# LayerNorm ahead of two feed-forwards: sums from the residual add and ScalarE's squares in place of VectorE's batch-norm statistics

## The chip, the cores and the metric

The kernel runs on one core of one Trainium2 chip. The metric is the device time of one execution in microseconds (us). The kernel before took 2121.43 us (median of three runs, 2121.37 to 2122.96). The engines are named as in the profile: PE is TensorE's matrix multiplication and PEld its weight load, DVE is VectorE, ACT is ScalarE, POOL is GpSimd, SP is the engine whose queue issues most of the DMAs.

## The reference

A decoder of two layers on 1024 positions of width 1024, all in float32. Each layer is a token mixer (a gated linear recurrence in the first, sliding-window attention in the second) and a gated feed-forward with a convolution of width 3. After the mixer and after the feed-forward stands a residual sum with a LayerNorm. The change touches the LayerNorm between mixer and feed-forward, once in each layer:

```
def layer_norm(x, g, b):
    mu = xf.mean(-1, keepdims=True)
    var = jnp.square(xf - mu).mean(-1, keepdims=True)
    y = (xf - mu) * lax.rsqrt(var + LN_EPS) * g + b

for layer in range(DEPTH):
    mix = ...
    h = layer_norm(ALPHA * h + mix, ln_mix_g[layer], ln_mix_b[layer])
    ff = conv_ffn(h, ffn_w_in[layer], ffn_conv_w[layer], ffn_conv_b[layer], ffn_w_out[layer])
    h = layer_norm(ALPHA * h + ff, ln_ffn_g[layer], ln_ffn_b[layer])
```

## The kernel before

Float32 products are computed as three matrix products of a high and a low part (`mm3`, lines 222 to 224). The high part is a cast on ScalarE (line 249) and the low part a subtraction on VectorE (line 197), so every operand costs both engines an operation. The 1024 positions are eight blocks of 128 (`tb` 0 to 7), one position to a partition; a block's 1024 features lie in its row of `Y`.

The entry of a feed-forward is `out_proj`. It multiplies the mixer's output by its output weights in two passes over the blocks: first the left 512 columns for blocks 0 to 7, then the right 512 columns for blocks 4, 5, 6, 7, 0, 1, 2, 3. Each half is a group of 24 matrix products into one PSUM bank (`psmm`, a pool of four banks). At its end VectorE adds it to ALPHA times the residual (line 380, here called the block's sum) and so frees the bank, and takes batch-norm statistics of that half (line 263). After the right half follows the norm of that block, `Up.ln`: aggregate the statistics (line 269), add the epsilon (line 270), raise to the power -1/2 on GpSimd (line 271), subtract the mean and multiply by `g` (line 280, the first pass), multiply by the root and add `b` (line 283, the second pass). Some 8 to 13 us later by the planner's count, TensorE transposes the block (line 232) into two more PSUM banks, from which ScalarE and VectorE make the high and low parts of `T`; sums of parts that the feed-forward's fast matrix multiplication needs come from lines 433 to 445. Between these stand the first weights of the feed-forward: loads on SP, casts on ScalarE, sums on VectorE (lines 480 to 483).

The order of TensorE's work is written out by hand through `Order`, which steps generators as its own clock `t` advances. The order of ScalarE's, VectorE's, GpSimd's and SP's work in the entries is set by the framework's scheduler, which goes by its own costs; operations in `urgent()` come ahead of others. Each engine then runs its list strictly in order.

Of the kernel before, what the change touches and what calls it, by code (L numbers as in the profile page):

```python
# [10 lines left out]
F32 = mybir.dt.float32  # L11
# [5 lines left out]
P = 128  # L17
S = 1024
D = 1024
# [115 lines left out]
def trunk(ctx: ExitStack, tc: tile.TileContext, a: dict, out: bass.AP):  # L135
# [123 lines left out]
    def ln_half(tb, i):  # L259

        if tb not in half_stats:
            half_stats[tb] = sm.tile([P, 2, 6], F32, name="st", bufs=8)
        nc.vector.bn_stats(half_stats[tb][:, i, :], Y[:, tb, i * 512:(i + 1) * 512])  # L263
# [7 lines left out]
        nc.gpsimd.tensor_tensor(rs, rs, nhalf, op=ALU.pow)  # L271
        return mv, rs

    def ln_affine(tb, rows, dst, n=1):

        y = Y[:, tb, :]
        mv, rs = ln_stats(tb)
        parts = [slice(h * D // n, (h + 1) * D // n) for h in range(n)]
        for hs in parts:
            nc.vector.scalar_tensor_tensor(y[:, hs], y[:, hs], mv[:, 0:1], rows[0][:, hs],  # L280
                                           op0=ALU.subtract, op1=ALU.mult)
        for hs in parts:
            nc.vector.scalar_tensor_tensor(y[:, hs], y[:, hs], rs, rows[1][:, hs], op0=ALU.mult, op1=ALU.add)  # L283
            nc.sync.dma_start(dst(hs), y[:, hs])
# [71 lines left out]
    def out_proj(us, begun, rows, resid, ff, ln):  # L356
        tasks, late = [], []
        for tb in range(NB):
            nc.sync.dma_start(Y[:, tb, :], resid(tb))
        for tb, ps in enumerate(begun):  # L360
            out_part(ps, us, tb, [KC - 1])
        for dh in range(2):
            if dh:
                ff.row_loads()
                ff.weights(1)
            for tb in range(NB):
                if dh == 0 and tb < 4:
                    out_late(late, rows, tb, ff.TX)
                elif dh == 0 and tb == 4:
                    ff.weights(0)  # L370
                if dh:
                    tb = (tb + 4) % NB
                if dh == 0 and tb < len(begun):
                    ps = begun[tb]
                else:
                    ps = psmm()
                    out_part(ps, late if dh else us, tb, range(KC))
                y = Y[:, tb, dh * 512:(dh + 1) * 512]
                with urgent() if dh else nullcontext():
                    nc.vector.scalar_tensor_tensor(y, y, ALPHA, ps, op0=ALU.mult, op1=ALU.add)  # L380
                    ln_half(tb, dh)
                if dh == 1:
                    tasks.append(od.spawn(ln(tb)))
                    od.tick()
        return tasks
# [17 lines left out]
    class Up:  # L403
        def __init__(self, l, pool, rx):
            self.l, self.rx = l, rx
            self.wv = a["ffn_w_in"][l].rearrange("(kc p) c -> p kc c", p=P)
            self.TX = pool.tile([P, 2, 2, 4, 512], F32R, name="TX")
            self.T2 = pool.tile([P, 2, 4, 512], F32R, name="T2")
            self.W, self.raw, self.pieces = {}, {}, 0

        def row_loads(self):
# [5 lines left out]

        def ln(self, tb):
            with urgent():
                ln_affine(tb, self.rows, lambda hs: ynd[:, tb, hs], 2 if tb == 3 else 1)  # L420
            yield 8.0 if tb < 4 else 10.0 if self.l else 13.0
            turned = lambda t: (self.rx[2 * t - 4] if t in (2, 3) else Y[:, t, :]).rearrange("p (k t) -> p k t", k=KC)
            hf = turned(tb)
            ts = slice(tb * P, (tb + 1) * P)
            with urgent():
                for q in range(2):
                    ps, ks = psmm(), slice(4 * q, 4 * q + 4)
                    for k in range(4):
                        tr(ps[:, k * P:(k + 1) * P], Y[:, tb, (4 * q + k) * P:(4 * q + k + 1) * P])
                    pv = ps.rearrange("p (k t) -> p k t", k=4)  # L430
                    if tb < 4:
                        split(T[:, 0, ks, ts], T[:, 1, ks, ts], pv)
                        nc.scalar.copy(hf[:, ks], pv)
                    elif q == 0:
                        nc.scalar.copy(hf[:, ks], pv)
                    else:
                        split(T[:, 0, ks, ts], T[:, 1, ks, ts], pv)
                        tt(hf[:, ks], hf[:, :4], pv, op=add)
                        split(T[:, 0, :4, ts], T[:, 1, :4, ts], hf[:, ks])
                        return  # L440
            sf = turned(tb + 4)
            a11, a12, a21, s1 = hf[:, :4], hf[:, 4:], sf[:, :4], sf[:, 4:]
            tt(a21, a11, a21, op=sub)
            tt(a11, s1, a11, op=sub)
            tt(a12, a12, a11, op=sub)
            split(self.T2[:, 0, :, ts], self.T2[:, 1, :, ts], a21)
            yield 100.0
            pair = hf.rearrange("p (c k) t -> p c k t", c=2)
            split(self.TX[:, :, 0, :, ts], self.TX[:, :, 1, :, ts], pair)
# [1462 lines left out]
```

## Time and profile before

| | us |
|---|---|
| median of three runs | 2121.43 |
| the profiled execution | 2122.24 |
| its span, first to last instruction | 2120.4 |
| first entry, blocks' norms | about 498 to 555 from the span's start |
| second entry, blocks' norms | about 1437 to 1490 |

The profiled execution took 0.8 us more than the median. The page gives each engine's busy time, the chain of work that ended last and the costliest groups of instructions. A row of a group has the line of the kernel, the engine, the operation, output and inputs, the shape, the count, busy time, the mean in ns, and the idle time of the engine just before these instructions with what ended it. A row in order of time has its start, its duration, the engine, the line and the operation; in brackets stands how long the engine had been idle and for what.

### The profile page before, as it was taken

Reading aid. Unit: us, or ns where it says so; the run is one execution under the profiler, and the core shown is the slowest. Engines: PE = TensorE matmul, PEld = TensorE weight load, DVE = VectorE, ACT = ScalarE, POOL = GpSimd, SP = SyncE. Lnnn points to the kernel's source line nnn. Section 1 sums busy time; section 2 is a strip of 40 time slices with the busy share of each in tenths; the row PEclk is TensorE's granted clock in tenths of the full one; section 3 lists DMA queues with packets and bytes.
Section 4 is the critical chain, followed back from the end, with each engine's and each line's share of the span. In section 5 each row is a group of like instructions: output and inputs, shape, how many; then the busy total and the mean of one; then the engine's idle time right before and its main releaser. Section 6 shows DMA issues by size and latency. Waiting matters only on the chain. (4 is left out here: it accounts for less than half of the span.)

```text
span 2120.4 us, 31566 instructions
## 1 busy us (share of the span) xinstructions
PE 2091.9 (99%) x12303; PEld 1742.8 (82%) x12303; DVE 1777.2 (84%) x2420; ACT 968.1 (46%) x1562; POOL 187.1 (9%) x214
## 2 busy tenths in 40 slices
PE   9899999999999999999999999999999999999998
PEld 7688888887878888888888888888888888888886
DVE  6677777769989999888988668979999999978986
ACT  6455565543444444444433356743544444444430
POOL 1000000001010000000001122311010000000002
PEclk9999999999999999999999999999999999999999
DMA  4021111143247765628754511052266776449662
GB/s 153 21 71 50 51 51 51 66 169 110 90 124 174 194 156 150 157 98 294 268 189 159 159 34 38 23 156 93 85 167 167 177 174 161 123 152 326 225 207 98
DMA packets 239823, 286.82 MB, mean 135 GB/s; under 512 B 30216, under 2 KB 160440, under 8 KB 239416
## 3 DMA queue, kind: packets, MB, share of 16 engines
q1 hardware_dynamic: 223360, 238.26, 34.6%
q0 software_dynamic: 15456, 46.16, 10.9%
q8 instruction: 97, 1.59, 0.3%
q14 instruction: 54, 0.44, 0.1%
q10 hardware_dynamic: 856, 0.37, 0.1%
HBM read 241.72 MB, written 89.15 MB: 156 GB/s over the span
## 5 line engine op out<-in xcount | busy, mean ns | idle before, releaser
L222 PE MATMUL psmm<-T,HL 128*128 128x512 f32 x816 | 323.3, 396 | 5.2 <-ACT T L874 4.8
L223 PE MATMUL psmm<-T,HL 128*128 128x512 f32 x816 | 319.2, 391 | 1.3 <-DVE T L197 1.3
L224 PE MATMUL psmm<-T,HL 128*128 128x512 f32 x816 | 319.3, 391 | 0.2 <-DVE HL L197 0.2
L528 DVE SCALAR_TENSOR_TENSOR Y<-Y,cwt,Y 128x1023 f32<-128x1023 f32 (+1 forms) x176 | 225.1, 1281 | 49.7 <-ACT Y L526 48.3
L249 ACT CAST HL<-rx 128x1024 fp32r<-128x1024 f32 (+1 forms) x151 | 151.1, 1006 | 159.6 <-DMA rx<-in_ffn_w_in_dram 28.1
L197 DVE TENSOR_TENSOR HL<-rx,HL 128x1024 fp32r<-128x1024 f32 (+1 forms) x151 | 176.4, 1175 | 17.6 <-ACT HL L249 17.3
L222 PEld LDWEIGHTS psmm<-T,HL 128*128 128x128 f32 x816 | 153.9, 189 | 36.8 <-ACT T L874 5.2
L224 PEld LDWEIGHTS psmm<-T,HL 128*128 128x128 f32 x816 | 153.8, 188 | 33.0 <-DVE HL L197 0.6
L223 PEld LDWEIGHTS psmm<-T,HL 128*128 128x128 f32 x816 | 153.9, 189 | 32.8 <-DVE T L197 2.2
L222 PE MATMUL psax<-T,HL 128*128 128x512 f32 x392 | 153.5, 392 | 0.0
L223 PE MATMUL psax<-T,HL 128*128 128x512 f32 x392 | 152.9, 390 | 0.0
L224 PE MATMUL psax<-T,HL 128*128 128x512 f32 x392 | 152.7, 390 | 0.0
L526 ACT ACTIVATE Y<-Y,cwt 128x1024 f32<-128x1024 f32 x88 | 108.8, 1237 | 92.8 <-DVE Y L515 82.8
L197 DVE TENSOR_TENSOR HL<-raw,HL 128x512 fp32r<-128x512 f32 (+1 forms) x121 | 92.2, 789 | 40.6 <-ACT HL L1296 30.7
L271 POOL TENSOR_TENSOR rs<-rs,nhalf 128x1 f32<-128x1 f32 x32 | 45.0, 1407 | 735.3 <-DVE rs L270 735.3
L249 ACT CAST HT<-rx 128x1024 fp32r<-128x1024 f32 (+1 forms) x37 | 35.5, 960 | 139.2 <-DVE rx L482 61.9
L222 PEld LDWEIGHTS psax<-T,HL 128*128 128x128 f32 x392 | 73.8, 188 | 15.9 <-ACT Y L507 0.4
L222 PE MATMUL psmm<-HL 128*128 128x512 f32 x220 | 86.9, 395 | 0.0
L224 PEld LDWEIGHTS psax<-T,HL 128*128 128x128 f32 x392 | 73.8, 188 | 15.4
L223 PEld LDWEIGHTS psax<-T,HL 128*128 128x128 f32 x392 | 73.8, 188 | 15.2
L223 PE MATMUL psmm<-HL 128*128 128x512 f32 x220 | 85.9, 391 | 0.0
L224 PE MATMUL psmm<-HL 128*128 128x512 f32 x220 | 85.8, 390 | 0.0
(404 smaller groups left out, 5200.5 us busy)
## 6 DMA issues: line engine op xcount, KB each, us to landing
rx<-in_ffn_w_in_dram SPq DMA_DIRECT2D x136, 256.0 KB
rx<-gd SPq DMA_DIRECT2D x118, 256.0 KB
bsd<-in_ffn_w_out_dram POOLq DMA_DIRECT2D x36, 768.0 KB, 8.4
gd<-Y SPq DMA_DIRECT2D x44, 512.0 KB
raw<-in_hgrn_w_in_dram SPq DMA_DIRECT2D x30, 512.0 KB
rx<-in_ffn_w_out_dram SPq DMA_DIRECT2D x54, 256.0 KB
R<-bsd SPq DMA_DIRECT2D x44, 256.0 KB
Y<-in_ffn_w_in_dram SPq DMA_DIRECT2D x40, 256.0 KB
```

Of the source, the lines that this page charges most:

```text
L197: make = lambda e: e.tensor_tensor(lo, src, hi.bitcast(F32), op=ALU.subtract)
L222: nc.tensor.matmul(ps, st(0), mv(0), start=start, stop=False, skip_group_check=onto)
L223: nc.tensor.matmul(ps, st(0), mv(1), start=False, stop=False, skip_group_check=onto)
L224: nc.tensor.matmul(ps, st(1), mv(0), start=False, stop=stop, skip_group_check=onto)
L249: nc.scalar.copy(hi, src)
L271: nc.gpsimd.tensor_tensor(rs, rs, nhalf, op=ALU.pow)
L526: nc.scalar.activation(c, u, AF.Identity, bias=cwt[:, l, 3, ci:ci + 1], scale=cwt[:, l, 2, ci:ci + 1])
L528: nc.vector.scalar_tensor_tensor(c[:, sh:], u[:, :S - sh], cwt[:, l, 2 - sh, ci:ci + 1], c[:, sh:], op0=ALU.mult, op1=ALU.add)
```

## The change

For the two norms ahead of the feed-forwards, the residual sum also writes the sum of its 512 outputs per row (`accum_out`). From the two sums VectorE makes minus the mean (`less`). ScalarE squares each half with that as its bias and writes the sum of the squares; the squares themselves go to a scratch tile that nothing reads. VectorE adds the two sums and divides by 1024, GpSimd adds the epsilon in an operation of its own and raises to the power. The first pass adds `less` where it subtracted the mean. The norms after the feed-forwards keep the statistics.

```
+    def summed_half(tb, i, ps):
+        if tb not in half_stats:
+            half_stats[tb] = sm.tile([P, 2, 6], F32, name="st", bufs=8)
+        y = Y[:, tb, i * 512:(i + 1) * 512]
+        nc.vector.scalar_tensor_tensor(y, y, ALPHA, ps, op0=ALU.mult, op1=ALU.add,
+                                       accum_out=half_stats[tb][:, 0, i:i + 1])
+
+    def square_stats(tb, scratch):
+        st = half_stats.pop(tb)
+        less = st[:, 0, 2:3]
+        rs = sm.tile([P, 1], F32, name="rs")
+        nc.vector.tensor_scalar(less, st[:, 0, 0:1], st[:, 0, 1:2], -1.0 / D, op0=ALU.add, op1=ALU.mult)
+        for i in range(2):
+            nc.scalar.activation(scratch, Y[:, tb, i * 512:(i + 1) * 512], AF.Square, bias=less,
+                                 accum_out=st[:, 1, i:i + 1])
+        nc.vector.tensor_scalar(rs, st[:, 1, 0:1], st[:, 1, 1:2], 1.0 / D, op0=ALU.add, op1=ALU.mult)
+        nc.gpsimd.tensor_scalar(rs, rs, 1.0, LN_EPS, op0=ALU.mult, op1=ALU.add)
+        nc.gpsimd.tensor_tensor(rs, rs, nhalf, op=ALU.pow)
+        return less, rs
...
-    def ln_affine(tb, rows, dst, n=1):
+    def ln_affine(tb, rows, dst, n=1, scratch=None):
-        mv, rs = ln_stats(tb)
+        if scratch is None:
+            mv, rs = ln_stats(tb)
+            mean, from_it = mv[:, 0:1], ALU.subtract
+        else:
+            mean, rs = square_stats(tb, scratch)
+            from_it = ALU.add
...
-            nc.vector.scalar_tensor_tensor(y[:, hs], y[:, hs], mv[:, 0:1], rows[0][:, hs],
-                                           op0=ALU.subtract, op1=ALU.mult)
+            nc.vector.scalar_tensor_tensor(y[:, hs], y[:, hs], mean, rows[0][:, hs],
+                                           op0=from_it, op1=ALU.mult)
...
-                y = Y[:, tb, dh * 512:(dh + 1) * 512]
-                    nc.vector.scalar_tensor_tensor(y, y, ALPHA, ps, op0=ALU.mult, op1=ALU.add)
-                    ln_half(tb, dh)
+                    summed_half(tb, dh, ps)
...
+            self.scratch = pool.tile([P, 512], F32, name="sq")
```

In the changed kernel's lines, the sum is line 279, minus-mean 287, the squares 289, the small operation 291, the first pass 307, the second pass 310; the low part of a transposed block is still line 197, and a sum of parts is 464 (438 before).

VectorE in the second entry, from the sum of block 5 to the second pass that follows block 6's; before:

```order
L380 SCALAR_TENSOR_TENSOR Y1_4374<-Y1_4374,psmm_11986 128x512
L197 TENSOR_TENSOR HL_84<-rx2_11787,HL_84 128x1024
L263 BN_STATS st_11875<-Y1_4374 128x6
L269 BN_AGGR mv_12013<-st_11875 128x2
L270 TENSOR_SCALAR rs_12014<-mv_12013 128x1
L280 SCALAR_TENSOR_TENSOR Y1_4374<-Y1_4374,mv_12013,HL_84 128x1024
L380 SCALAR_TENSOR_TENSOR Y1_4374<-Y1_4374,psmm_12021 128x512
L283 SCALAR_TENSOR_TENSOR Y1_4374<-Y1_4374,rs_12014,rx1_11786 128x1024
L263 BN_STATS st_11903<-Y1_4374 128x6
```

And in the changed kernel (`psmm_11981` is block 5's right half, `psmm_12017` block 6's):

```order
L279 SCALAR_TENSOR_TENSOR Y1_4374,st_11871<-Y1_4374,psmm_11981 128x512
L287 TENSOR_SCALAR st_11871<-st_11871 128x1
L291 TENSOR_SCALAR rs_12007<-st_11871 128x1
L307 SCALAR_TENSOR_TENSOR Y1_4374<-Y1_4374,st_11871,HL_84 128x1024
L310 SCALAR_TENSOR_TENSOR Y1_4374<-Y1_4374,rs_12007,rx1_11787 128x1024
L279 SCALAR_TENSOR_TENSOR Y1_4374,st_11898<-Y1_4374,psmm_12017 128x512
L197 TENSOR_TENSOR T_81<-psmm_12048,T_81 128x4x128
L287 TENSOR_SCALAR st_11898<-st_11898 128x1
```

Block 6's sum moved from ahead of block 5's second pass to behind it, and between block 5's sum and its second pass nothing of another block is left.

ScalarE in the second entry, around block 6's transposes and block 0's norm; before:

```order
L435 COPY Y1_4374<-psmm_12145 128x512
L249 CAST T_81<-psmm_12151 128x4x128
L249 CAST T_81<-Y1_4374 128x4x128
L435 COPY Y1_4374<-psmm_12196 128x512
L249 CAST T_81<-psmm_12202 128x4x128
```

And in the changed kernel (`st_11827` holds block 0's sums, the two `psmm` of the first rows hold block 6's transposes):

```order
L461 COPY Y1_4374<-psmm_12143 128x512
L249 CAST T_81<-psmm_12149 128x4x128
L289 ACTIVATE sq_11794,st_11827<-Y0_4181,st_11827 128x512
L249 CAST T_81<-Y1_4374 128x4x128
L289 ACTIVATE sq_11794,st_11827<-Y0_4181,st_11827 128x512
L461 COPY Y1_4374<-psmm_12195 128x512
L249 CAST T_81<-psmm_12201 128x4x128
```

The two squares of block 0 stand among the casts of block 6, with one cast between them.

VectorE in the first entry, from block 6's sum to block 7's; before:

```order
L283 SCALAR_TENSOR_TENSOR Y1_4374<-Y1_4374,rs_4919,rx1_4699 128x1024
L380 SCALAR_TENSOR_TENSOR Y1_4374<-Y1_4374,psmm_4926 128x512
L197 TENSOR_TENSOR HL_84<-rx0_4698,HL_84 128x512
L263 BN_STATS st_4808<-Y1_4374 128x6
L480 TENSOR_TENSOR rx2_4700<-rx0_4698,rx2_4700 128x512
L269 BN_AGGR mv_4953<-st_4808 128x2
L481 TENSOR_TENSOR rx0_4698<-rx0_4698 128x512
L270 TENSOR_SCALAR rs_4954<-mv_4953 128x1
L280 SCALAR_TENSOR_TENSOR Y1_4374<-Y1_4374,mv_4953,HL_84 128x1024
L197 TENSOR_TENSOR T_81<-psmm_4983,T_81 128x4x128
L283 SCALAR_TENSOR_TENSOR Y1_4374<-Y1_4374,rs_4954,rx1_4699 128x1024
L380 SCALAR_TENSOR_TENSOR Y1_4374<-Y1_4374,psmm_4961 128x512
```

And in the changed kernel (`psmm_4921` is block 6's right half, `psmm_4957` block 7's):

```order
L279 SCALAR_TENSOR_TENSOR Y1_4374,st_4802<-Y1_4374,psmm_4921 128x512
L310 SCALAR_TENSOR_TENSOR Y1_4374<-Y1_4374,rs_4911,rx1_4699 128x1024
L287 TENSOR_SCALAR st_4802<-st_4802 128x1
L197 TENSOR_TENSOR HL_84<-rx0_4698,HL_84 128x512
L506 TENSOR_TENSOR rx2_4700<-rx0_4698,rx2_4700 128x512
L507 TENSOR_TENSOR rx0_4698<-rx0_4698 128x512
L291 TENSOR_SCALAR rs_4947<-st_4802 128x1
L307 SCALAR_TENSOR_TENSOR Y1_4374<-Y1_4374,st_4802,HL_84 128x1024
L197 TENSOR_TENSOR T_81<-psmm_4979,T_81 128x4x128
L310 SCALAR_TENSOR_TENSOR Y1_4374<-Y1_4374,rs_4947,rx1_4699 128x1024
L279 SCALAR_TENSOR_TENSOR Y1_4374,st_4829<-Y1_4374,psmm_4957 128x512
```

Block 5's second pass moved from ahead of block 6's sum to behind it, and the small operation (line 291) now stands two operations behind minus-mean, with the squares on ScalarE in between. TensorE's order is the same in both kernels.

More of the change, by code (lines that the diff above doesn't have):

```diff
@@ L419, in ln @@
             with urgent():
-                ln_affine(tb, self.rows, lambda hs: ynd[:, tb, hs], 2 if tb == 3 else 1)
+                ln_affine(tb, self.rows, lambda hs: ynd[:, tb, hs], 2 if tb == 3 else 1, self.scratch)
             yield 8.0 if tb < 4 else 10.0 if self.l else 13.0
```

## The prediction

> **What bounds the kernel now.** I read the page's busy times first, then the stages, then who waits for whom, and last single instructions in order of time.
>
> ```profile
> PE 2091.9 (99%) x12303; PEld 1742.8 (82%) x12303; DVE 1777.2 (84%) x2420; ACT 968.1 (46%) x1562; POOL 187.1 (9%) x214
> ...
> 500.00:546.00 46.00, 42.52 (x210) 34.99 (x209) 45.42 (x71) 16.51 (x26) 10.28 (x7) 1.00 0.24 92
> ...
> 1437.00:1485.00 48.00, 48.00 (x241) 40.36 (x241) 46.00 (x75) 16.58 (x28) 10.42 (x8) 1.00 0.19 77
> ```
>
> TensorE is the bound, and nothing taken from another engine counts unless TensorE waits for that engine. The two stage rows are the entries of the two feed-forwards, where the change works (columns: length, busy us of PE, PEld, DVE, ACT, POOL, granted clock, DMA share, GB/s). VectorE is nearly full in both (45.42 of 46, 46.00 of 48). Only in the first does TensorE have gaps, 46.00 less 42.52 = 3.5 us; in the second it has none. Its waits from 498 to 560 us say whom it waits for (total, times, longest):
>
> ```profile
> PE psmm L232 <- DVE Y L380: 1.6, 1, 1.6
> PE psmm L232 <- ACT Y L433: 1.2, 1, 1.2
> PE psmm L232 <- DVE Y L438: 0.4, 1, 0.4
> ```
>
> All are the transposes of line 232, waiting for a PSUM bank that VectorE or ScalarE has yet to empty. So less work on VectorE can win at most these 3.5 us, 0.16% of the time. A difference of 0.2%, 4.2 us, is about what a measurement of this kernel can tell from no change.
>
> **The change part by part.** Removed, for each of 16 blocks: two statistics, their aggregate and the old small operation. From the groups of the second entry (count, busy us, mean ns):
>
> ```profile
> L263 DVE BATCH_NORM_STATS2 st<-Y 128x6 f32<-128x512 f32 x8 | 5.5, 687 | 0.0
> ...
> L269 DVE BATCH_NORM_AGGREGATE mv<-st 128x2 f32<-128x12 f32 x8 | 1.6, 205 | 0.1
> L270 DVE TENSOR_SCALAR rs<-mv 128x1 f32<-128x1 f32 x8 | 1.2, 147 | 0.0
> ```
>
> This is up to 2 x 0.69 + 0.20 us of VectorE per block. Added there: one more 128x1 operation (0.15), and reading out the sum, twice. Added on ScalarE: two squares of 128x512, each with its read-out. Added on GpSimd: one 128x1 operation ahead of the power. None of the added operations is on VectorE's path alone: they make a chain through three engines, and VectorE stands at both ends of it. This is how one turn of the chain goes now, in the second entry, from the residual sum of block 0 to that of block 1, with GpSimd's power in the last row (start, duration):
>
> ```profile
> 1462.82 0.68 DVE L380 SCALAR_TENSOR_TENSOR Y<-Y,psmm 128x512 f32<-128x512 f32 x1
> ...
> 1464.01 0.69 DVE L263 BATCH_NORM_STATS2 st<-Y 128x6 f32<-128x512 f32 x1
> ...
> 1465.41 0.15 DVE L270 TENSOR_SCALAR rs<-mv 128x1 f32<-128x1 f32 x1
> 1465.47 1.27 DVE L280 SCALAR_TENSOR_TENSOR Y<-Y,mv,HL 128x1024 f32<-128x1024 f32 x1
> 1467.19 1.28 DVE L283 SCALAR_TENSOR_TENSOR Y<-Y,rs,rx 128x1024 f32<-128x1024 f32 x1 [0.44 <-POOL rs L271]
> ...
> 1469.05 0.68 DVE L380 SCALAR_TENSOR_TENSOR Y<-Y,psmm 128x512 f32<-128x512 f32 x1
> ...
> 1465.70 1.46 POOL L271 TENSOR_TENSOR rs<-rs,nhalf 128x1 f32<-128x1 f32 x1 [4.72 <-DVE rs L270]
> ```
>
> TensorE's transposes in the same stretch:
>
> ```profile
> 1460.37 1.03 PE L232 MATMUL psmm<-ident,Y 128*128 128x128 f32 x8
> ...
> 1466.70 1.03 PE L232 MATMUL psmm<-ident,Y 128*128 128x128 f32 x8
> ...
> 1470.32 1.03 PE L232 MATMUL psmm<-ident,Y 128*128 128x128 f32 x8
> ```
>
> The reader is to see that the turn takes 6.23 us (1469.05 - 1462.82) and already contains a wait of 0.44 us for GpSimd, while TensorE needs a block every 6.33 us (1466.70 - 1460.37). The chain is just fast enough: 0.1 us to spare. The transposes at 1470.32 are block 0's; they need its second pass, done at 1467.19 + 1.28 = 1468.47, so they have 1.85 us in hand.
>
> The new pieces have no row of their own in this stage. The nearest rows:
>
> ```profile
> 1300.28 0.39 ACT L1714 ACTIVATE X<-X,nm 128x129 f32<-128x129 f32 x1
> 1300.58 0.19 ACT L1714 ACTIVATION_READ_ACCUMULATOR X<-X,nm 128x1 f32 x1
> 1300.67 0.39 ACT L1714 ACTIVATE X<-X,nm 128x129 f32<-128x129 f32 x1
> ...
> 378.66 0.62 ACT L1296 CAST HL<-raw 128x512 fp32r<-128x512 f32 x1 [1.61 <-DVE raw L1319]
> ...
> 379.19 0.63 ACT L1395 ACTIVATE VG<-VG 128x512 f32<-128x512 f32 x1
> ...
> 468.00 0.20 POOL L1234 TENSOR_SCALAR ss<-ss 128x8 f32<-128x8 f32 x1 [44.97 <-ACT sq L1233]
> 468.28 1.64 POOL L1235 TENSOR_TENSOR ss<-ss,nhalf 128x8 f32<-128x8 f32 x1
> ...
> L1234 POOL TENSOR_SCALAR ss<-ss 128x8 f32<-128x8 f32 x8 | 3.6, 454 | 440.2 <-ACT sq L1233 440.2
> ```
>
> - A square with its read-out: an activation over 129 elements that gives a sum comes round every 0.39 us (1300.67 - 1300.28). An operation over 512 elements takes a slot of 0.53 (379.19 - 378.66), and 0.19 for the read-out bounds it above by 0.72, below by 0.53. I take 0.71, since the read-out is a row of its own; a pair is 1.42.
> - GpSimd's added operation: 0.28 us from its start to the power's (468.28 - 468.00); the mean of the group is 0.45. Bounds 0.2 and 0.45; I take 0.28, the row in which nothing else was late.
> - Reading the sum out on VectorE: no row. Not below nothing, as it adds an output and takes away no work of the instruction; ScalarE's 0.19 from above, unless the read-out slows the stream itself (second rival). I take 0.15.
> - Each handoff between engines: 0.1 us, an estimate from the rows above (the power ends at 1467.16, the second pass starts at 1467.19; rs ends at 1465.56, the power starts at 1465.70).
>
> **The new turn.** From block 0's sum, the new order on VectorE is: sum 0.60, low part of a transposed block 0.60, minus-mean 0.15 plus read-out and handoff, so ScalarE's first square starts 1.5 us in. ScalarE has a cast (0.53) between the two squares: 1.5 + 0.71 + 0.53 + 0.71 = 3.45. Handoff and the small operation to 3.65, GpSimd 0.1 + 0.28 + 1.46 + 0.1 to about 5.5, second pass 1.2 to 6.7. The turn grows from 6.23 to 6.7 and TensorE's pace of 6.33 is missed by 0.4 to 0.5 a block. VectorE works less in it and waits more, at the small operation (for ScalarE) and at the second pass (for GpSimd). Queued behind both is the next block's sum, which empties a PSUM bank.
>
> The turn from block 5 to 6 suffers most:
>
> ```profile
> 1445.36 0.69 DVE L380 SCALAR_TENSOR_TENSOR Y<-Y,psmm 128x512 f32<-128x512 f32 x1
> ...
> 1449.33 0.68 DVE L380 SCALAR_TENSOR_TENSOR Y<-Y,psmm 128x512 f32<-128x512 f32 x1
> 1449.92 1.28 DVE L283 SCALAR_TENSOR_TENSOR Y<-Y,rs,rx 128x1024 f32<-128x1024 f32 x1
> ```
>
> Before, block 6's sum stands ahead of block 5's second pass, 3.97 us after block 5's sum. In the new order it stands behind it, with nothing between to fill the waits: 0.68 + 0.15 + 0.15 + 0.1, squares 1.42, 0.1 + 0.15, GpSimd 1.95, second pass 1.2 = 5.9 us. Block 5's own sum comes about 1.1 late (0.6 for one subtraction that now precedes block 4's sum, 0.5 for block 4's longer turn). So block 6's sum is 1.1 + 1.9 = 3.0 late, and block 0's some 3.4. Block 0's second pass is 3.4 + (5.5 - 4.37) = 4.5 late, against 1.85 in hand: TensorE waits 2.6 us at the transposes that stood at 1470.32. From there TensorE goes with the chain: block 1 comes another 0.4 over its pace and block 2 some 0.2, while block 3, whose sum stands ahead of block 2's second pass, adds nothing. **Second entry: +3.2 us**, where before there was no gap.
>
> First entry, blocks 6 and 7:
>
> ```profile
> 511.33 0.68 DVE L380 SCALAR_TENSOR_TENSOR Y<-Y,psmm 128x512 f32<-128x512 f32 x1
> ...
> 516.31 1.27 DVE L283 SCALAR_TENSOR_TENSOR Y<-Y,rs,rx 128x1024 f32<-128x1024 f32 x1
> 517.50 0.68 DVE L380 SCALAR_TENSOR_TENSOR Y<-Y,psmm 128x512 f32<-128x512 f32 x1
> ...
> 518.24 0.66 PE L232 MATMUL psmm<-ident,Y 128*128 128x128 f32 x4 [1.64 <-DVE Y L380]
> ```
>
> Here VectorE runs behind, and the removed statistics help: block 6's sum comes about 2.0 earlier (the last statistics and aggregates of blocks 4 and 5, 1.4 start to start, and block 5's second pass, 1.2, that now follows it, less 0.6 for the added small operations and read-outs). The turn from 6 to 7 then grows from 6.17 to 7.4 (it holds block 5's second pass, the new chain and its own second pass), so block 7's sum comes 0.8 earlier and the 1.64 us wait shrinks to 0.8; the 0.4 us wait goes too. That is 1.2 won. Three further turns, each longer than TensorE's pace by 0.4, give it back, so the waits at blocks 0 and 1 return at the old times; block 3 adds 0.3. **First entry: +0.3 us.**
>
> Everything else I cost at nothing. VectorE's saving of some 18 us is outside TensorE's waits; ScalarE's 32 squares are about 23 us on an engine 46% busy; GpSimd waits most of the time for this chain. On SP a few weight loads of the first entry trade places, and in the second the load of one row of the norm, at a DMA share of 0.24 and 0.19; if that cover failed, a wait for a load would show on ScalarE. Sum: 2122.24 + 3.2 + 0.3 = 2125.7 for the profiled execution, which took 0.8 more than the median of the runs; from the median, **2125.0 us**.
>
> **The rivals.**
> - *The relief pays and the chain hides.* If the handoffs are shorter, or the sums come early enough that the chain's extra runs while TensorE still computes, the 3.4 us of waits (1.6 + 1.2 + 0.4 and a remainder of 0.2) go and none comes: 2121.4 - 3.4 = 2118.0. For it: VectorE is full in both entries. Against: the 0.44 us wait for GpSimd shows that the turn is bound by the chain already. It decides if the new turn is under 6.3 us. Chance 0.13.
> - *The sum is read out at the cost of a second pass* over the data (0.6 more per sum, what a statistic cost start to start): every turn 0.6 longer. Six turns in the second entry, 3.6, and the first entry's relief with its later turns, about 3.0: 2125.0 + 6.6 = 2131.6. What the trace has of this instruction, without a read-out:
>
> ```profile
> L380 DVE SCALAR_TENSOR_TENSOR Y<-Y,psmm 128x512 f32<-128x512 f32 x8 | 5.4, 680 | 0.0
> ...
> L280 DVE SCALAR_TENSOR_TENSOR Y<-Y,mv,HL 128x1024 f32<-128x1024 f32 (+1 forms) x9 | 10.3, 1157 | 0.0
> ```
>
>   With one input in PSUM (L380) it takes 0.68 for 512 elements, with both in SBUF (L280) 1.2 for 1024, so inputs do not slow it; what a read-out does, no row says. It decides if a sum takes over 1.0 us. Chance 0.12. [...]
> - *ScalarE is late.* Its queue is in order, and squares stand behind casts of transposed blocks:
>
> ```profile
> ACT T L249 <- PE psmm L232: 5.9, 5, 1.7
> ```
>
>   Those casts waited 1.2 us each for TensorE in the first entry. A square held 0.5 us in each of some nine turns gives 4.5 more: 2129.5. It decides once squares start over 0.5 us after minus-mean. Chance 0.30, and slower than before by over 0.2%.
> - *The change doesn't do what it says* is left out: the order shows the statistics gone and the squares there.
>
> **How the numbers follow.** My forecast, a loss of 0.5 to 4.2 us, has 0.45. With the rivals: slower by over 0.2%: 0.30 + 0.12 = 0.42; faster by over 0.2% needs more than all waits of the first entry, 0.05 of the first rival's 0.13; within 0.2% 0.45 + 0.08 = 0.53. The range goes from 2119, short of the first rival, to 2131, near the second.
>
> **What would show it.** In the changed kernel's second entry: gaps of TensorE before the transposes of block 0, about 2.6 us; a turn of 6.7 us from block 0's sum to block 1's; VectorE idle for ScalarE at the small operation and for GpSimd at the second pass, some 1 to 2 us a block. In the first: the 1.64 us wait at half, and waits at blocks 0 and 1 as before. Wrong would be: no gap in the second entry (the chain hides), a residual sum much over 0.68 us (the read-out costs), or waits for weights.

## The result, and the profile after

The changed kernel took 2125.78 us (median of 14 runs, 2123.95 to 2128.26), the kernel before 2121.17 in as many on the same chips (2119.53 to 2124.32). The ratio is 1.0022, with a 95% interval of 1.0015 to 1.0030: 4.6 us slower. The forecast was 2125.0. The profiled execution has a span of 2124.4 us, against 2120.4 before.

The page's busy times:

```profile
PE 2093.5 (99%) x12303; PEld 1741.7 (82%) x12303; DVE 1762.6 (83%) x2420; ACT 988.1 (47%) x1626; POOL 192.0 (9%) x230
```

The same two stage rows as before (length, busy us of PE, PEld, DVE, ACT, POOL, granted clock, DMA share, GB/s):

```profile
500.00:546.00 46.00, 42.10 (x202) 34.78 (x201) 42.09 (x69) 26.06 (x54) 12.96 (x13) 0.96 0.24 92
1437.00:1485.00 48.00, 45.42 (x218) 37.77 (x217) 38.02 (x65) 22.98 (x50) 11.41 (x14) 0.96 0.16 66
```

VectorE lost 14.6 us of work (1777.2 to 1762.6), and in the second entry 8 of its 46. TensorE, which had no gap there, now has 2.6 us of them (48.00 less 45.42), fewer products in the same stretch (218 after 241), and a granted clock of 0.96 in both entries. Whom it waits for, in the first entry (498 to 560 us) and in the second (1437 to 1500):

```profile
PE psmm L232 <- DVE Y L310: 2.3, 2, 2.0
PE psmm L232 <- DVE Y L279: 1.9, 1, 1.9
...
PE psmm L232 <- DVE Y L310: 2.6, 1, 2.6
```

The waits for an empty bank at the transposes (3.2 us in the first entry before) became waits for the second pass (line 310), the end of the new chain, and for the sum (line 279).

Where the 4 us of span arise is seen by following the same product or transpose through both traces (starts in us, and after less before):

| place | before | after | difference |
|---|---|---|---|
| ahead of the first entry's norms | 496.07 | 496.13 | +0.1 |
| last transposes of the first entry | 546.61 | 548.82 | +2.2 |
| behind before's wait at 612 us | 618.73 | 616.49 | -2.2 |
| first layer's feed-forward, from here constant | 673.36 | 672.60 | -0.8 |
| block 6's transposes, second entry | 1466.70 | 1465.90 | -0.8 |
| behind the second entry | 1486.59 | 1490.61 | +4.0 |

Three things happened: the first entry lost 2.2 us, the stretch behind it won 4.4 and gave 1.5 back, and the second entry lost 4.8. The turn of the chain in the second entry, from block 0's sum to block 1's, on VectorE, then ScalarE and GpSimd:

```profile
1465.13 0.68 DVE L279 SCALAR_TENSOR_TENSOR Y<-Y,psmm 128x512 f32<-128x512 f32 x1
1465.74 0.08 DVE L279 DVE_READ_ACCUMULATOR Y<-Y,psmm 128x1 f32 x1
...
1468.72 0.21 DVE L291 TENSOR_SCALAR rs<-st 128x1 f32<-128x1 f32 x1
1468.85 1.28 DVE L307 SCALAR_TENSOR_TENSOR Y<-Y,st,HL 128x1024 f32<-128x1024 f32 x1
1470.84 1.28 DVE L310 SCALAR_TENSOR_TENSOR Y<-Y,rs,rx 128x1024 f32<-128x1024 f32 x1 [0.71 <-POOL rs L293]
1472.04 0.68 DVE L279 SCALAR_TENSOR_TENSOR Y<-Y,psmm 128x512 f32<-128x512 f32 x1
...
1466.64 0.72 ACT L289 ACTIVATE sq<-Y,st 128x512 f32<-128x512 f32 x1 [3.90 <-DVE st L287]
...
1468.50 0.18 ACT L289 ACTIVATION_READ_ACCUMULATOR sq<-Y,st 128x1 f32 x1
...
1469.02 1.16 POOL L292 TENSOR_SCALAR rs<-rs 128x1 f32<-128x1 f32 x1 [5.12 <-DVE rs L291]
1470.26 0.55 POOL L293 TENSOR_TENSOR rs<-rs,nhalf 128x1 f32<-128x1 f32 x1
```

The turn takes 6.91 us (1472.04 - 1465.13), where it took 6.23 and TensorE needs a block every 6.33. TensorE at block 0's transposes and behind them:

```profile
1472.27 1.67 PE L232 MATMUL psmm<-ident,Y 128*128 128x128 f32 x8 [2.58 <-DVE Y L310]
1473.60 0.77 PE L222 MATMUL psmm<-TX,T 128*128 128x512 f32 x1
1474.17 0.63 PE L223 MATMUL psmm<-TX,T 128*128 128x512 f32 x1
...
1475.88 0.44 PE L224 MATMUL psmm<-TX,T 128*128 128x512 f32 x1
1476.16 0.40 PE L222 MATMUL psmm<-TX,T 128*128 128x512 f32 x1
```

The wait of 2.58 us has a tail: the eight transposes take 1.67 us where they took 1.03, and the products behind them start 0.43 us apart (0.23 otherwise) until 1475.9. These are called slow products below. The granted clock between 1472 and 1476 us is 0.57. Before's wait at 612 us had the same tail, and both are gone in the changed kernel:

```profile
612.20 0.50 PE L224 MATMUL psmm<-TX,HL 128*128 128x512 f32 x1 [2.68 <-DVE HL L197]
...
614.05 0.63 PE L224 MATMUL psmm<-TX,HL 128*128 128x512 f32 x1
614.48 0.63 PE L222 MATMUL psmm<-TX,HL 128*128 128x512 f32 x1
```

### The profile page after: what moved, and what is told of

It is laid out like the page before. It is cut to its first block, busy times and chain, and to the rows that moved or that the text cites. A ratio compares the mean times of both kernels' runs of the same rounds, so it can differ in the third digit from the quotient of the medians.

```text
span 2124.4 us, 31643 instructions
## 1 busy us (share of the span) xinstructions
PE 2093.5 (99%) x12303; PEld 1741.7 (82%) x12303; DVE 1762.6 (83%) x2420; ACT 988.1 (47%) x1626; POOL 192.0 (9%) x230
## 5 line engine op out<-in xcount | busy, mean ns | idle before, releaser
L249 ACT CAST HL<-Y 128x1024 fp32r<-128x1024 f32 (+1 forms) x32 | 28.5, 891 | 115.0 <-DVE Y L508 30.1
```

What stands on the lines that cost most here:

```text
L249: nc.scalar.copy(hi, src)
```

## The experiments

Each ratio is to the kernel before, run on the same chip in the same rounds; in brackets its 95% interval.

### Which entry costs: the change in one layer alone

```
-                    summed_half(tb, dh, ps)
+                    if ff.l == 0:      # 1 in the other kernel
+                        summed_half(tb, dh, ps)
+                    else:
+                        y = Y[:, tb, dh * 512:(dh + 1) * 512]
+                        nc.vector.scalar_tensor_tensor(y, y, ALPHA, ps, op0=ALU.mult, op1=ALU.add)
+                        ln_half(tb, dh)
...
-                ln_affine(tb, self.rows, lambda hs: ynd[:, tb, hs], 2 if tb == 3 else 1, self.scratch)
+                ln_affine(tb, self.rows, lambda hs: ynd[:, tb, hs], 2 if tb == 3 else 1, self.scratch if self.l == 0 else None)
```

> Only the first layer's entry has the change; the second keeps the batch-norm statistics. Theory A (the longer chain costs, the relief of VectorE pays later): TensorE is some 2.3 us late behind the first entry, wins it back and 3 more at the wait that stood at 612 us, and the second entry has no gap: 0.8 us faster than before. Theory B (the reordered loads and casts behind the first entry won time by chance, the chain alone decides): the same trace up to 1437 us, so this run tells A from B only by where the time goes; a loss of over 1 us would speak against both.

> Only the second layer's entry has the change. Theory A: a gap of 2.6 us before block 0's transposes and some 2 us of slow products behind it, nothing else: 4.7 us slower than before, more than the whole change. Rival (the loss comes from both entries alike): 2.3 us slower.

In the first entry alone: 2120.46 us after 2120.42, ratio 0.9999 [0.9990, 1.0008]. In the second alone: 2126.07, ratio 1.0026 [1.0015, 1.0038], 5.65 us slower: theory A's 4.7 lies in the interval, the rival's 2.3 does not. By these times the second entry makes the whole loss. The first alone loses 2.9 us at its transposes and wins them back at 612 us, as the changed kernel does; with the second alone the wait at 612 us stays (2.67 us), and block 0's transposes wait 2.5 us with the slow products behind.

### What the relief is worth, and what the load on ScalarE costs

Three kernels. One keeps the statistics and has ScalarE square the finished norm too, with sums that nothing reads:

```
+                unread = sm.tile([P, 2], F32, name="unread")
+                for i in range(2):
+                    nc.scalar.activation(self.scratch, Y[:, tb, i * 512:(i + 1) * 512], AF.Square,
+                                         accum_out=unread[:, i:i + 1])
```

> Both entries keep the statistics and get the same 32 squares on ScalarE as load alone: they read the finished norm, and nothing reads their sums. Theory A (waiting for the squares costs, not their work): within 1 us of before. Rival (ScalarE has no room for 23 us more in the entries, its casts come late): 3 to 5 us slower, with waits of TensorE for ScalarE.

It took 2128.27 us (four runs), ratio 1.0040 [1.0025, 1.0055]: 7.9 us slower, more than the rival's 3 to 5. And the trace has the loss elsewhere. TensorE's products in the first feed-forward, 720 to 1080 us, where no square runs (group, mean ns of one):

```profile
L222 PE MATMUL psmm<-T,HL 128*128 128x512 f32 x120 | 47.0, 392 | 0.0
L224 PE MATMUL psmm<-T,HL 128*128 128x512 f32 x120 | 46.9, 391 | 0.0
L223 PE MATMUL psmm<-T,HL 128*128 128x512 f32 x120 | 46.7, 389 | 0.0
```

They are 389 in each of the three lines before. Start to start a product takes 228.4 ns against 226.7 in 1600 products. The second kernel has the same squares, but their sums go into spare columns of the scratch tile:

```
-            self.scratch = pool.tile([P, 512], F32, name="sq")
+            self.scratch = pool.tile([P, 576], F32, name="sq")
...
-                unread = sm.tile([P, 2], F32, name="unread")
...
+                    nc.scalar.activation(self.scratch[:, :512], Y[:, tb, i * 512:(i + 1) * 512], AF.Square,
+                                         accum_out=self.scratch[:, 512 + i:513 + i])
```

> The kernel before with its statistics kept and the changed kernel's 32 squares on ScalarE, which read the finished norm and are not read, once more; but their sums now go into spare columns of the scratch tile, so that no tile of 8 bytes is added among the small ones. With that tile the feed-forward products of the first layer came 228.4 ns apart between 720 and 1080 us, against 226.7 before, which makes most of the 7.9 us that it was slower; at the entries themselves its TensorE lost under 1 us. Theory A (the load on ScalarE is hidden; the small tile slowed the products): 226.7 ns apart, within 1.5 us of before, 2119 to 2122. Theory B (the squares themselves slow what comes behind them): 228 ns apart again, 2126 to 2129.

2121.00 us, ratio 1.0001 [0.9992, 1.0010], products 226.7 ns apart: theory A. The squares as a load cost nothing that can be measured; the first kernel had measured its own extra tile.

The third keeps the sums with the residual and drops the squares (so it leaves the variance out; `rs` comes from the sums plus a constant):

```
-        for i in range(2):
-            nc.scalar.activation(scratch, Y[:, tb, i * 512:(i + 1) * 512], AF.Square, bias=less,
-                                 accum_out=st[:, 1, i:i + 1])
-        nc.vector.tensor_scalar(rs, st[:, 1, 0:1], st[:, 1, 1:2], 1.0 / D, op0=ALU.add, op1=ALU.mult)
-        nc.gpsimd.tensor_scalar(rs, rs, 1.0, LN_EPS, op0=ALU.mult, op1=ALU.add)
+        nc.vector.tensor_scalar(rs, st[:, 0, 0:1], st[:, 0, 1:2], 1.0e6, op0=ALU.add, op1=ALU.add)
```

> Leaves out the variance: sums as in the change, no squares, the root taken of the sums plus a constant, so VectorE has the relief without the long chain. Theory A: no gap in the second entry, under 1 us of the 3.5 us of gaps left in the first, and the wait that stood at 612 us gone: 6 to 9 us faster than before. Rival (relief of VectorE is worth nothing outside the first entry's gaps, as the prediction had it): at most 3.5 us faster.

2116.44 us, ratio 0.9981 [0.9972, 0.9990]. Its TensorE gains 3.2 us in the first entry and none in the second: there the relief alone is worth about what the prediction set as its bound, 3.5 us. Theory A's 6 to 9 us were missed, since the wait at 612 us, which it expected to go, stayed at 2.24 us with slow products behind it. So neither the load nor the relief makes the loss; the chain is left.

### What makes the chain long

All three have the change in the second entry alone, so the program up to there is that of before. First, GpSimd's added operation goes: the epsilon is added on VectorE, and the square takes a scaled mean, made by one more tiny VectorE operation.

```
+        nc.vector.tensor_scalar(st[:, 0, 3:4], st[:, 0, 0:1], st[:, 0, 1:2], -1.0 / (32.0 * D), op0=ALU.add, op1=ALU.mult)
...
-        nc.vector.tensor_scalar(rs, st[:, 1, 0:1], st[:, 1, 1:2], 1.0 / D, op0=ALU.add, op1=ALU.mult)
-        nc.gpsimd.tensor_scalar(rs, rs, 1.0, LN_EPS, op0=ALU.mult, op1=ALU.add)
+            nc.scalar.activation(scratch, Y[:, tb, i * 512:(i + 1) * 512], AF.Square, bias=st[:, 0, 3:4],
+                                 scale=1.0 / 32.0, accum_out=st[:, 1, i:i + 1])
+        nc.vector.tensor_scalar(rs, st[:, 1, 0:1], st[:, 1, 1:2], LN_EPS, op0=ALU.add, op1=ALU.add)
```

> The change in the second entry only (as in the run that gave 2126.07 us with a TensorE wait of 2.5 us at block 0's transposes), but with the epsilon added on VectorE and the mean scaled in the square, so that GpSimd's added operation leaves the chain and one tiny VectorE operation off the chain comes in. In the changed kernel the power ended 1.79 us after GpSimd began, against 1.45 for the power alone before: the turn should shrink by about 0.33 us, from 6.9 to 6.6. Theory A (the turn through ScalarE and GpSimd against TensorE's pace of 6.33, summed over some six turns, and a TensorE that goes slowly after a wait of 2 us or more): the wait at block 0's transposes falls from 2.5 to between 0.3 and 1.0 us, the slow products behind it go, the time is 2121 to 2123. Theory B (the squares wait on ScalarE behind the casts, and GpSimd's operation adds nothing): wait and time stay within 0.5 us of that run, 2126.

2125.86 us, ratio 1.0026 [1.0015, 1.0037]: the time of the second entry alone. The turn shrank by half of what was expected, from 6.91 to 6.76 us. The wait at block 0's transposes fell to 1.56 us and left no slow products. But TensorE, now earlier, met the next blocks' chains, still 0.4 us a turn over its pace: waits of 0.16, 0.50 and 0.37 us followed, and the second entry still cost 3.6 us (4.8 in the kernel with the second entry alone). Neither theory held whole: the slow products went, as theory A had it, but the wait stayed above its 0.3 to 1.0 us, and the time is theory B's.

Second, one more GpSimd operation stands ahead, beside the squares, and is not read:

```
+        nc.gpsimd.tensor_scalar(st[:, 0, 4:5], less, 1.0, 0.0, op0=ALU.mult, op1=ALU.add)
```

> The change in the second entry only, with one more operation on GpSimd per block, which reads minus the mean as soon as VectorE has it and whose result is not read; it runs beside the squares. In the changed kernel GpSimd's first operation after 5 us of idleness took 1.16 us and the power behind it 0.55, against 1.45 for the power alone as first operation before. Theory A1 (GpSimd needs some 0.9 us to start after idleness, whichever operation comes first): with the operation ahead the chain shortens by up to 0.9 us, the turn falls to about 6.1, the wait at block 0's transposes goes, 2120 to 2122. Theory A2 (the long time belongs to the operation that waits for another engine, idleness or not): the two operations on the chain take what they took, the wait stays at 2.0 to 2.8 us, 2125 to 2127.

2125.19 us, ratio 1.0023 [1.0013, 1.0033], wait 2.45 us: A2. GpSimd shows no start after idleness: the added operation takes 0.19 us after 2.74 us of it, and the one on the chain still 1.16. What the 1.16 us go with is seen in the same trace, where the operation ahead (line 291) runs once beside a VectorE operation with one input in PSUM and once beside one with both in SBUF:

```profile
1452.01 0.19 POOL L291 TENSOR_SCALAR st<-st 128x1 f32<-128x1 f32 x1 [2.74 <-DVE st L287]
...
1451.84 0.68 DVE L470 TENSOR_TENSOR Y<-Y,psmm 128x512 f32<-128x512 f32 x1
...
1480.80 0.56 POOL L291 TENSOR_SCALAR st<-st 128x1 f32<-128x1 f32 x1 [3.34 <-DVE st L287]
...
1480.63 0.68 DVE L476 TENSOR_TENSOR Y<-Y,Y 128x512 f32<-128x512 f32 x1
```

The same operation takes 0.19 us beside line 470, and beside line 476 it ends 0.05 us after that operation (1481.36 and 1481.31). The one in the chain runs beside the first pass (line 307, two inputs in SBUF) and ends 0.05 us after it (1470.18 and 1470.13 in the changed kernel); at all sixteen blocks of the changed kernel it ends 0.04 to 0.05 us after a VectorE operation with two inputs in SBUF.

Third, the variance comes from the mean of squares less the square of the mean. A half's square needs no mean and starts when its sum ends:

```
         nc.vector.scalar_tensor_tensor(y, y, ALPHA, ps, op0=ALU.mult, op1=ALU.add,
                                        accum_out=half_stats[tb][:, 0, i:i + 1])
+        nc.scalar.activation(sqs[0], y, AF.Square, scale=1.0 / 32.0, accum_out=half_stats[tb][:, 1, i:i + 1])
...
+        nc.vector.scalar_tensor_tensor(st[:, 0, 3:4], less, less, epst, op0=ALU.mult, op1=ALU.subtract)
+        nc.vector.scalar_tensor_tensor(rs, st[:, 1, 0:1], st[:, 1, 1:2], st[:, 0, 3:4], op0=ALU.add, op1=ALU.subtract)
         nc.gpsimd.tensor_tensor(rs, rs, nhalf, op=ALU.pow)
```

> The change in the second entry only, but with the variance from the mean of squares less the square of the mean: the square of a half needs no mean, so it starts when its sum ends; three tiny VectorE operations, GpSimd with the power alone. Chain after a block's sum: sum 0.7, square and read-out 0.7, small operation and handoffs 0.4, power 1.45, second pass 1.2: about 4.6 us, under TensorE's pace of 6.33 for a block. Theory A: no wait over 0.5 us at the second entry's transposes and no loss there; 2119.5 to 2121.5, as before. Theory B (ScalarE's queue holds the squares back behind casts, which end only when TensorE has transposed): waits of 1 to 3 us remain, 2122 to 2126.

2121.88 us, ratio 1.0006 [0.9996, 1.0015], no wait in the second entry, and the same product 1.9 us earlier than before's ahead of it and behind it, so nothing is lost there (1.7 of the 1.9 are there at 200 us already, where the two programs differ by one constant at most): theory A, with a median 0.4 us over the range that it gave. The turn is 5.9 us. GpSimd's power in this kernel, first beside the first pass, then beside a subtraction with two SBUF inputs, then beside one from PSUM:

```profile
1449.71 1.46 POOL L293 TENSOR_TENSOR rs<-rs,nhalf 128x1 f32<-128x1 f32 x1 [3.14 <-DVE rs L292]
1458.55 0.87 POOL L293 TENSOR_TENSOR rs<-rs,nhalf 128x1 f32<-128x1 f32 x1 [7.38 <-DVE rs L292]
...
1477.20 0.55 POOL L293 TENSOR_TENSOR rs<-rs,nhalf 128x1 f32<-128x1 f32 x1 [6.05 <-DVE rs L292]
```

The first ends 0.41 us after the first pass beside it (1451.17 and 1450.76), the second 0.41 us after its subtraction (1459.42 and 1459.01), and the third takes 0.55 us. By these rows some 0.9 of the power's 1.46 us in the kernel before (1.46 less 0.55) are waiting for the first pass beside it, which is an estimate. By it, leaving out GpSimd's other operation (0.19 us by itself) could not win the 1.16 us of its row.

### What made the wait at 612 us vanish

TensorE waited there for a low part on VectorE (line 197, `HL<-Y,HL`). Before, it starts at 610.94, in the changed kernel at 603.63:

```profile
608.01 1.27 DVE L528 SCALAR_TENSOR_TENSOR Y<-Y,cwt,Y 128x1022 f32<-128x1022 f32 x1
609.21 0.67 DVE L520 TENSOR_TENSOR Y<-Y,psax 128x512 f32<-128x512 f32 x1
609.81 1.21 DVE L197 TENSOR_TENSOR HL<-rx,HL 128x1024 fp32r<-128x1024 f32 x1
610.94 1.21 DVE L197 TENSOR_TENSOR HL<-Y,HL 128x1024 fp32r<-128x1024 f32 x1
```

```profile
603.63 2.84 DVE L197 TENSOR_TENSOR HL<-Y,HL 128x1024 fp32r<-128x1024 f32 x1
606.39 1.21 DVE L197 TENSOR_TENSOR HL<-rx,HL 128x1024 fp32r<-128x1024 f32 x1
607.52 1.27 DVE L554 SCALAR_TENSOR_TENSOR Y<-Y,cwt,Y 128x1023 f32<-128x1023 f32 x1
608.72 1.21 DVE L544 TENSOR_TENSOR Y<-Y,psmm 128x1024 f32<-128x1024 f32 x1
```

It lasts 2.84 us where the row behind it takes 1.21; a GpSimd operation (line 559) runs beside it until 605.38. The low part is not only earlier: the build put it ahead of the convolution's passes and of emptied banks that stood ahead of it before. VectorE's order there is the same in the changed kernel and in that with the first entry alone, and both lack the wait; it is that of before in the kernels with the second entry alone, and all have it (2.7 to 2.8 us). Relief alone does not remove it: the kernel without squares has the relief in both entries, between 585 and 612 us VectorE's order of before, and a wait of 2.24 us there. To test order without relief, the kernel before gets those operations earlier in the framework's list, by 60, 100 or 300 places, and nothing else:

```
                 if fc > 2:
-                    self.weights(fc)
+                    with tc.high_priority(offset=60) if fc == 3 and self.l == 0 else nullcontext():
+                        self.weights(fc)
```

> The kernel before, with the operations that make the weights of slice 3 of the first layer's feed-forward put 60 places ahead in the framework's order: the low part for which TensorE waits 2.68 us at 612 us stands ahead of four operations of the convolution and of an emptied bank. Nothing else of the change. Theory A (in the changed kernel that wait vanished because its build orders VectorE's work behind the first entry in another way, not because VectorE was relieved): the wait at 612 falls below 0.5 us, with the slow products behind it 4 us are won, less up to 1.5 given back at the next products; 2116 to 2118.5. Theory B (the wait goes because VectorE has less to do in the entry before): the wait stays, or another of the same size takes its place within 100 us; 2120 to 2121.

2119.35 us, ratio 0.9996 [0.9986, 1.0005], between the ranges of the two theories. In the trace, which is of the slowest of its ten runs (2116.40 to 2121.11), the wait at 612 us went, as theory A had it, and one of the same size came at 635, as theory B had it:

```profile
635.53 0.63 PE L222 MATMUL psax<-T,HL 128*128 128x512 f32 x1 [2.28 <-ACT Y L507]
635.95 0.63 PE L223 MATMUL psax<-T,HL 128*128 128x512 f32 x1
```

The same product was 0.7 us earlier than before's ahead of 612 us, 4.9 between the two waits, and 0.7 behind the second. Was it this order, or does VectorE need the relief?

> The kernel before with its statistics, and the weights of slice 3 in the first layer put 100 places ahead in place of 60: another order of VectorE's and ScalarE's work between 585 and 640 us, and no relief of VectorE in the entry. With 60 places the wait of 2.7 us at 612 went and one of 2.3 us came at 635, for a copy on ScalarE; in the kernel with the variance from the mean of squares no wait over 0.3 us is left there. Theory A (which wait stands there is a matter of the build's order alone): with some order no wait over 1 us is left between 600 and 640, and 3 to 4.5 us are won, 2116.5 to 2118.5. Theory B (VectorE is too late there without its relief in the entry, so that a wait only moves): the waits there add up to 2 us or more again, 2119 to 2121.5.

> The same with 300 places, the offset of the program's other urgent operations. Theory A: as in the run with 100 places, no wait over 1 us between 600 and 640 in at least one of the two, 2116.5 to 2118.5. Theory B: waits of 2 us or more in both, 2119 to 2121.5.

2117.88 us, ratio 0.9989 [0.9980, 0.9998], and 2117.77, ratio 0.9984 [0.9974, 0.9993]. The waits left between 595 and 720 us are 0.9 and 0.6 us in the one, 1.2 in the other. Both times are theory A's: the order alone wins about 3 us there, and no relief is needed. (That no wait over 1 us is left, which it expected of at least one of the two, holds for the first only.)

### The version that beats both

> Both entries with the variance from the mean of squares less the square of the mean, so that each square starts when its half's sum ends and GpSimd has the power alone. In the second entry alone this cost nothing: its turn there was 5.9 us (from the sum at 1461.25 to that at 1467.15), under TensorE's pace of 6.33. In the first entry the kernel without squares had 0.3 us of waits left at the transposes, where the kernel before has 3.4. Theory A (the relief of VectorE is worth the first entry's waits once the chain no longer lengthens the turn): under 1 us of waits at the first entry's transposes and none in the second, 2 to 3 us faster than before, 2117 to 2119. Theory B (what is won ahead of 600 us is lost at the weights behind it, for which TensorE waits in all kernels): the waits go, but the time is that of before, 2120 to 2122. Whether a wait of over 2 us behind 600 us is there and is followed by slow products moves either by up to 2 us.

The mean of squares in both entries: 2116.29 us (11 runs) against 2121.09, ratio 0.9978 [0.9970, 0.9987], 4.8 us faster than before. But not as theory A had it: the first entry keeps waits of 2.0, 0.6 and 0.5 us and wins nothing (the same product 0.7 us earlier ahead of it and behind it). The gain is made behind it: the build's order leaves 0.3 us of waits between 595 and 720 us, and the same product is 4.7 us earlier there. What this version does for the second entry is to cost nothing. Another order of VectorE's work alone, without any change to the norms, came to 0.9984 [0.9974, 0.9993], so that the new norm itself wins anything is not shown.

## Why the prediction was right, and where it was not

**The second entry, forecast +3.2, measured +4.8.** The mechanism held: the chain is over TensorE's pace, and TensorE waits for it at block 0's transposes, 2.58 us for a forecast of 2.6. From block 0's sum the first square was to start 1.5 us in and started 1.51 in (1466.64); the small operation was to be done at 3.65, and the first pass behind it starts at 3.72; the second pass, due at 5.5, came at 5.71; the turn of 6.7 was 6.91. VectorE's idle time for ScalarE stands one operation ahead of where it was forecast: the low part at 1468.00 waits 0.86 us for the cast between the squares. Of the prices, the square's 0.71 was 0.72 with a cast behind it (0.85 with the second square right behind it), the read-out's 0.15 was a row of 0.08. The sum stayed at 0.68, so the rival of the second pass over the data fell. GpSimd's added operation at 0.28 cost 0.33 (1469.02 to the power's end at 1470.81 is 1.79, against 1.46): right in size, for a reason that the prediction did not have. Its row ends 0.05 us after the first pass (1470.18 and 1470.13), as the power before ended 0.42 us after it (1467.16 and 1466.74), so by the estimate above both rows hold a wait for that pass.

That the wait came out so exactly is in part luck. Measured against TensorE, which is 0.8 us ahead in this trace, block 5's sum was 0.2 us late and not 1.1 (at 1444.71, before at 1445.36), block 6's 2.2 and not 3.0, block 0's 3.1 and not 3.4. The longer way from block 0's sum to its second pass made up for it, and that pass was 4.5 late, as forecast.

The term that was mis-sized is what comes behind block 0: 0.6 was forecast, and 2.2 measured. The turn from block 1's sum to block 2's took 7.51 us (1472.04 to 1479.55; 6.25 before), 1.2 over TensorE's pace where 0.2 was forecast. In the changed kernel most of the 2.2 us shows as slow transposes (0.6) and slow products (1.2), and a wait of only 0.13 is left at block 2. But the slow products do not make the loss. The kernel with one more GpSimd operation has the same chain (that turn takes 7.50 us) and a wait of 2.45 us at block 0, and its clock stayed at 1.00 (the stretch 1472 to 1476 us, in the columns of the stage rows above):

```profile
1472.00:1476.00 4.00, 3.98 (x22) 3.35 (x22) 3.12 (x8) 2.70 (x7) 0.52 (x2) 1.00 0.34 135
```

Its TensorE's waits from 1400 to 1540 us (total, times, longest):

```profile
PE psmm L232 <- DVE Y L311: 3.0, 3, 2.5
PE psmm L232 <- ACT Y L465: 0.5, 1, 0.5
```

It lost 4.5 us in the second entry all the same (0.9 us earlier than before at block 6's transposes, 3.6 later behind the entry): where nothing was slow, TensorE waited 0.28, 0.50 and 0.32 us at blocks 1 and 2. So the slow products stand for the most part where TensorE would have waited, and add some 0.4 us (4.83 less 4.47, one trace of each).

**The first entry, forecast +0.3, measured +2.2.** "Block 6's sum comes about 2.0 earlier" failed: it came 0.9 earlier, at 510.43. VectorE stood still ahead of it for a load:

```profile
507.92 1.28 DVE L310 SCALAR_TENSOR_TENSOR Y<-Y,rs,rx 128x1024 f32<-128x1024 f32 x1 [1.73 <-DMA rx<-in_ln_mix_b_dram]
...
510.43 0.68 DVE L279 SCALAR_TENSOR_TENSOR Y<-Y,psmm 128x512 f32<-128x512 f32 x1
...
517.80 0.68 DVE L279 SCALAR_TENSOR_TENSOR Y<-Y,psmm 128x512 f32<-128x512 f32 x1
```

The row `b` of the norm lands then. Its load is issued when VectorE has made the low part `HT` of line 197, at 504.35 (505.09 before), and lands 3.6 us later; the pass was ready at 506.2. Before, VectorE came to this pass at 508.94 and did not notice. The prediction asked whether loads would be late, but not whether a pass that is ready 2.7 us earlier would meet a load that comes only 0.7 earlier. The turn from 6 to 7 was 7.37 us, as forecast (7.4), so block 7's sum came 0.3 late and not 0.8 early (517.80), the wait there was 1.88 and not 0.8, and block 0's transposes waited 2.02 us, with slow products again (granted clock 0.61 between 533 and 537 us). (Between minus-mean and the small operation of block 6 stand three operations, lines 197, 506 and 507, and not two.)

**"Everything else I cost at nothing"** was wrong by -3.0 us. The order behind the entries was compared only where the change works; the scheduler had also moved some thirty VectorE operations between 575 and 680 us, and the wait at 612 us, with its slow products, fell out. So the total is 0.8 us off by the medians and 0.5 by the two profiled spans, but it holds errors of +1.6, +1.9 and -3.0. That these nearly cancel is luck: none of the three terms had its size right, and only the second entry's had its mechanism right.

**The rivals.** The relief does not pay because the chain is over TensorE's pace, as the forecast had it; with a chain of 5.9 us the loss in the second entry is gone. ScalarE's queue held squares back less than that rival needs: the first square started within 0.1 us of minus-mean in nine of the sixteen blocks, 0.4 us after it in four, and over 0.5 us (0.51, 0.86, 0.92) in three. At block 0 of the second entry ScalarE waited 3.90 us for minus-mean.

## What to carry to other kernels

Work that is taken off a full engine and handed through two others is priced by the turn of the chain against the pace of the engine that bounds, not by the busy time saved; take the operations off the chain that need not wait (here the square that needs no mean). An edit under a scheduler also reorders what it does not touch, so compare the order on every engine up to where the two programs agree again, and look at each wait of TensorE in that stretch: one wait there was worth 3 us, where the change cost 4.6. Work that comes earlier must be checked against the loads that do not come as much earlier.

## What the runs showed of the hardware that was not expected

- Behind some waits of TensorE of 2 to 3 us its products are slow. In the changed kernel the granted clock is 0.50 from 533.90 to 537.31 us, behind the wait of 2.02 us, and from 1472.57 to 1475.98, behind that of 2.58; in the kernel before it is 0.50 from 613.29 to 616.70, behind the wait of 2.68 us at 612. Each of the three stretches is 3.41 us long, with 1.00 on either side of it. In the kernel with the second entry alone the clock is 0.74 from 1472 to 1476 us and 0.83 from 1476 to 1480, behind a wait of 2.5, and in the one with weights 60 places ahead 0.59 from 635 to 639, behind 2.28. But the length of a wait does not tell by itself: that of 2.45 us in the kernel with one more GpSimd operation left the clock at 1.00 from 1472 to 1476. It stayed at 1.00 for 4 to 5 us behind waits of 1.56 us (the kernel without GpSimd's added operation, from 1472), 1.64 (before, from 518) and 1.88 (the changed kernel, from 518) as well. What decides it is not shown.
- GpSimd's small operations took longer beside a VectorE operation with two inputs in SBUF, and ended shortly after it: one took 0.19 us beside an operation with an input in PSUM, and 0.56, to 0.05 us after the end, beside one with both in SBUF; the power took 0.55 us beside the former kind, and 0.87 or 1.46, to 0.41 us after the end, beside the latter.
- An added tile of 8 bytes a partition went with 1.7 ns more a product (228.4 against 226.7 ns between 720 and 1080 us), by estimate 6 us over the feed-forwards. That the addresses of other tiles moved is a possible reason; it was not tried by itself.
